# Squares of the keys two slots earlier, scaled keys one later, output transposes behind the inversion's products

## The chip, the cores and the metric

The kernel runs on one core of a Trainium2 chip. The metric is the device time of one execution in microseconds (us); the time before is the median of three runs. A profiled execution of the same program gives the trace that is read here. Engines are called PE (TensorE matmul), PEld (its weight loads), DVE (VectorE), ACT (ScalarE), POOL (GpSimd) and SP (SyncE, which issues the DMAs).

## The reference, cut to what matters

Two layers over 256 positions of width 2048. Each layer normalises, projects by one matrix, and feeds two groups of heads: RWKV-7 time mixing in both directions (16 heads of 64), and windowed attention. Both are gated, concatenated and projected back. The change is in the time mixing; cut to its core:

```python
kk = heads(kf * k_k)
kk = kk * lax.rsqrt(jnp.maximum(jnp.sum(kk * kk, -1, keepdims=True), 1e-24))
for d, rev in enumerate((False, True)):
    ...                                   # decay, a, kd by low-rank products
    y = y + wkv_scan(rh, heads(decay), kd, vh, kk, heads(a), rev)
    bonus = bonus + jnp.sum(rh * kd * rkf, -1, keepdims=True)
mu = jnp.mean(y, -1, keepdims=True)
var = jnp.mean(jnp.square(y - mu), -1, keepdims=True)
yn = (y - mu) * lax.rsqrt(var + LNX_EPS)
out = yn * lnx_g + lnx_b + bonus * vh
...
S = S * w_t - s_kk * (a_t * kk_t) + v_t * k_t     # one step of the scan
```

The squares of the scaled keys and their sum over a head are the first line's norm; the normed output `yn` is what the transposes turn back.

## The kernel before, in words

All activations lie transposed, channels on partitions. The big projections stream weights of 128 x 1024 floats. Each is split by ACT into a high part (`hi`, line 241) and by DVE into a low part (`lo`, line 243), and each of a projection's 16 steps is three matmuls (lines 311 to 313). PE is nearly always in this stream; everything else is put between its steps.

The time mixing works on eight pairs of heads per layer, with chunks of 64 positions. Three generators hold its steps, one step from one `yield` to the next:

- `scan_p` (line 710): squares of the keys (`sq` on ACT, in the trace `t`; high copy `mf` on ACT; low part `sl` on DVE), scaled keys `kkr` (line 722), head sums `pk` on PE (lines 706 and 727), reciprocal and `kd` on DVE (line 730), then decays, key and value products, `vt` and its copies `suv` (lines 795 and 798), and the bonus sums `pbn`.
- `scan_i`: the chunk matrices (line 829) and their inversion in six levels, each a pair of steps: products `pq` (line 927) with a copy `QF` on ACT, and products `pd` (line 936) with a predicated copy on DVE.
- `scan_b`: the chunk recurrence, then the norm of the outputs: squares on ACT (line 1031), a power on POOL, the product `ysq` on DVE (line 1035), the transposes (line 1040, in the trace `py<-C,ysq`), and the gate.

The function `window` (line 413) runs 64 steps of the projection stream in 11 slots, five or six in each. Ahead of a slot's steps it advances the generators that have that slot in their list, in the order in which `scans` gives them. Window w starts `scan_p` for pair w, goes on with it for pair w - 1, runs `scan_i` for w - 2 and w - 3, and `scan_b` for w - 3 and w - 4. A pair's own projections run in its window: keys end in slot 2, values in slot 5, receptance in slot 8, gate in slot 10. A layer has twelve windows with such work and one with attention alone.

PE's order is this program order exactly (`manual_schedule`). On ACT, DVE and POOL a scheduler orders by readiness and priority when the program is built; afterwards each engine keeps that order. Steps issued through `PA` and `PV` (line 256, the helper's line in the trace) keep their program order among themselves on ACT and on DVE; `high_priority` moves others ahead, all of `scan_b` among them. SP issues the weight loads, which wait for free buffers.

PSUM for these products comes from two pairs of banks in turn (`wpair`, `wbank`), so a product may wait until what was read from an earlier one is done. `kkr`, `mf` and `sl` have one buffer each, the tag `t1` (squares, and the gated outputs) three.

Of the kernel before, what the change touches and what calls it, by code (L numbers as in the profile page):

```python
# [9 lines left out]
F32 = mybir.dt.float32  # L10
# [6 lines left out]
ALU = mybir.AluOpType  # L17
# [25 lines left out]

SLOTS = 11

STAGE_P = (([8], [6, 7, 8, 10]), ([9], [0, 1, 3, 4, 5, 6, 7, 8, 9]))
STAGE_I = (list(range(SLOTS)), [0, 1, 2, 3, 4])
STAGE_B = (list(range(5, SLOTS)), list(range(SLOTS)))
ATT = [
    [3, 9],  # L50
    [1, 3, 5, 6, 8, 10],
# [82 lines left out]
def hybrid_trunk_kernel(ctx, tc, xT, wi, wv, wo, par, fing, dup, iup, sink, pos, cst, out):  # L134
# [24 lines left out]
    def st(tag, shape, dt=F32, bufs=1):  # L159
        return sp.tile([128, *shape], dt, tag=tag, name=tag, bufs=bufs)  # L160
# [97 lines left out]
    PA, PV = InTurn(A), InTurn(V)  # L258
# [415 lines left out]
    def layer(l):  # L674
# [33 lines left out]


        def scan_p(p, t):  # L710
            K, VV = t["k"], t["v"]
            two = lambda x: x.unsqueeze(1).to_broadcast([128, 2, T])
            dd = lambda x: x.rearrange("p (d x) -> p d x", d=2)
            c8 = lambda x: x.rearrange("p (n j) -> p n j", j=64)
# [2 lines left out]
            sq = st("t1", [T], bufs=3)  # L717
            PA.activation(sq, K, AF.Square, scale=prm(P_KK, p))
            square = (st("mf", [T], F32R), st("sl", [T], F32R))
            PA.activation(square[0], sq, AF.Copy)  # L720
            KR = st("kkr", [T])
            PA.activation(KR, K, AF.Identity, scale=prm(P_KK, p))
            yield
            PV.tensor_tensor(square[1], sq, square[0].bitcast(F32), op=ALU.subtract)
            yield
            pk = wbank("pk")
            head_sums(pk, square)
# [2 lines left out]
            PV.reciprocal(KD, pk[:, 0:T])  # L730
            PV.scalar_tensor_tensor(KD, KD, 1e24, KR, op0=ALU.min, op1=ALU.mult)
            yield
# [40 lines left out]
            PA.activation(BK8[64:128, :, 0, :], BK8[64:128, :, 2, :], AF.Copy)  # L773
            yield

            R = t["r"]
            MV = st("mv", [2, NC, 2, 64], bufs=3)
            kr4 = c4(KR)
            PV.scalar_tensor_tensor(MV[:, 0, :, 0, 1:64], PP[:, 0, :, 0:63], -1.0, kr4[:, :, 1:64], op0=ALU.mult, op1=ALU.mult)
# [6 lines left out]
            PV.tensor_tensor(km[:, 0:T], km[:, 0:T], km[:, T : 2 * T], op=ALU.add)  # L786
            PV.scalar_tensor_tensor(km[:, 0:T], km[:, 0:T], prm(P_RK, p), R, op0=ALU.mult, op1=ALU.mult)
            yield
            PV.tensor_tensor(MV[:, :, :, 1, :], c4(R).unsqueeze(1).to_broadcast([128, 2, NC, 64]), PP, op=ALU.mult)
            SUV = st("suv", [2, NC, 2, 64], bufs=3)  # L790
# [263 lines left out]
        def scans(w):  # L1054

            gens = []
            prep = [(1, STAGE_P[1]), (0, STAGE_P[0])]
            stages = [(lag, scan_p, at[0]) for lag, at in prep]
            stages += [(4, scan_b, STAGE_B[1]), (3, scan_i, STAGE_I[1]), (2, scan_i, STAGE_I[0])]
            stages += [(3, scan_b, STAGE_B[0])]  # L1060
            stages += [(lag, scan_p, at[1]) for lag, at in prep]
            for lag, scan, at in stages:
                p = w - lag
                if 0 <= p < NP:
                    if (scan, p) not in chains:
                        chains[scan, p] = scan(p, L.ts[p])
                    gens.append((chains[scan, p], at))
            return gens
# [75 lines left out]
        for w in range(NP + 2):  # L1144
            window(64, *scans(w), *([(setup_, ROT.get(w, [2, 5, 9, 9]))] if l == 0 else []))
        att = attend()
        window(64, *scans(NP + 2), (att, ATT[0]))
        window(64, *scans(NP + 3), (att, ATT[1]))
        window(64, (att, ATT[2]))
        for _ in att:  # L1150
# [130 lines left out]
```

## Time and profile before

| | |
|---|---|
| median of three runs | 1194.66 us (1192.85 to 1195.58) |
| the profiled execution | 1198.96 us |
| its span, first to last instruction | 1197.2 us |
| mean granted PE clock | 0.987 |
| PE busy | 1159.4 us, 97% |
| PEld busy | 1084.0 us, 91% |
| DVE busy | 909.8 us, 76% |
| ACT busy | 778.6 us, 65% |
| DMA queue of the weights, share of 16 engines | 42.9% |

In the trace's lines an operation is given as out<-in by the program's tile names; `L706` is line 706 of the kernel. A timeline's line begins with its start and its duration in us, and a bracket at its end gives the idle time of the engine before it and what ended that.

### The profile page before, as it was taken

The numbers are of one execution on the slowest core, as the hardware profiler recorded it, in microseconds if no ns is written. First come the engines' busy times: TensorE is split into PE (matmuls) and PEld (weight loads), VectorE is DVE, ScalarE is ACT, GpSimd is POOL, SyncE is SP. The second block draws the span as 40 slices with busy tenths as digits, with TensorE's granted clock in tenths as the row PEclk, the third lists the DMA queues.
The fourth block names the chain that finished last, engine by engine and source line by source line (L and its number), as shares of the span: only waits on it lengthen the run. The fifth ranks groups of instructions, "written<-read, shape, count | busy, mean of one in ns | idle before, by whom it ended". The sixth has DMA issues, their size and how long they took to land.

```text
span 1197.2 us, 38092 instructions
## 1 busy us (share of the span) xinstructions
PE 1159.4 (97%) x16151; PEld 1084.0 (91%) x16151; DVE 909.8 (76%) x2017; ACT 778.6 (65%) x1955; POOL 22.2 (2%) x23
## 2 busy tenths in 40 slices
PE   8999999999999999999999999999999999999996
PEld 6988898889899988999999889898889999989996
DVE  6888978888777677856668888877887766786554
ACT  6657767776775667655556577867776666675553
POOL 0000000000000000000000000000000000000000
PEclk8999999999999999999999999999999999999998
DMA  7543333333233433477655343333333344345663
GB/s 255 163 148 127 110 119 98 121 98 114 90 108 123 136 116 117 140 222 246 203 186 181 117 136 105 110 115 108 114 97 108 116 139 133 98 147 184 209 191 122
DMA packets 60410, 166.63 MB, mean 139 GB/s; under 512 B 7728, under 2 KB 22736, under 8 KB 60240
## 3 DMA queue, kind: packets, MB, share of 16 engines
q1 hardware_dynamic: 60240, 164.21, 42.9%
q8 instruction: 126, 2.06, 0.7%
q14 instruction: 44, 0.36, 0.1%
HBM read 157.37 MB, written 4.19 MB: 135 GB/s over the span
## 4 chain that ended last, share of the span: by engine, by line
PE 69%; issue 14%; ACT 9%; DVE 5%; DMA 2%; SPq 0%; POOL 0%; POOLq 0%; DVEq 0%; ACTq 0%
PE pm L311 17%; PE pm L313 14%; PE pm L312 14%; PE pg L829 3%; ACT hi L241 3%; PE pcc L992 2%; PE py L1004 1%; PE py L977 1%; PE pd L936 1%; PE pcc L1020 1%; DVE kd L256 1%; DVE lo L243 1%; PE pcc L1010 1%; PE pq L927 1%; ACT suv L798 1%
## 5 line engine op out<-in xcount | busy, mean ns | idle before, releaser
L243 DVE TENSOR_TENSOR lo<-raw,hi 128x512 fp32r<-128x512 f32 x560 | 370.8, 686 | 123.7 <-ACT hi L241 118.5
L241 ACT ACTIVATE hi<-raw 128x512 fp32r<-128x512 f32 x560 | 330.3, 624 | 202.9 <-PE pm L312 110.7
L311 PE MATMUL pm<-XHa,hi 128*128 128x256 f32 x832 | 248.7, 299 | 1.7 <-ACT XHa L203 1.1
L311 PE MATMUL pm<-XHb,hi 128*128 128x256 f32 x832 | 244.1, 293 | 0.1
L312 PE MATMUL pm<-XLa,hi 128*128 128x256 f32 x832 | 236.2, 284 | 0.5 <-DVE XLa L204 0.3
L313 PE MATMUL pm<-XHb,lo 128*128 128x256 f32 x832 | 234.3, 282 | 1.7 <-DVE lo L243 1.7
L313 PE MATMUL pm<-XHa,lo 128*128 128x256 f32 x832 | 235.3, 283 | 0.0
L312 PE MATMUL pm<-XLb,hi 128*128 128x256 f32 x832 | 234.2, 282 | 0.0
L311 PEld LDWEIGHTS pm<-XHa,hi 128*128 128x128 f32 x832 | 158.9, 191 | 14.1 <-issue 3.2
L311 PEld LDWEIGHTS pm<-XHb,hi 128*128 128x128 f32 x832 | 157.5, 189 | 6.1 <-ACT hi L241 0.3
L312 PEld LDWEIGHTS pm<-XLa,hi 128*128 128x128 f32 x832 | 159.4, 192 | 1.1 <-DVE XLa L204 1.1
L313 PEld LDWEIGHTS pm<-XHb,lo 128*128 128x128 f32 x832 | 157.5, 189 | 2.1 <-DVE lo L243 2.1
L313 PEld LDWEIGHTS pm<-XHa,lo 128*128 128x128 f32 x832 | 159.2, 191 | 0.0
L312 PEld LDWEIGHTS pm<-XLb,hi 128*128 128x128 f32 x832 | 157.7, 190 | 0.3 <-DVE XLb L204 0.3
L1015 ACT ACTIVATE suv<-pcc 64x128 f32<-64x128 f32 x128 | 34.5, 270 | 72.9 <-PE pcc L1013 49.3
L311 PE MATMUL pm<-MHa,hi 128*128 128x256 f32 x256 | 72.2, 282 | 0.0
L313 PE MATMUL pm<-MHa,lo 128*128 128x256 f32 x256 | 72.0, 281 | 0.2 <-DVE lo L243 0.2
L312 PE MATMUL pm<-MLb,hi 128*128 128x256 f32 x256 | 71.9, 281 | 0.0
L311 PE MATMUL pm<-MHb,hi 128*128 128x256 f32 x256 | 71.9, 281 | 0.0
L313 PE MATMUL pm<-MHb,lo 128*128 128x256 f32 x256 | 71.9, 281 | 0.0
L312 PE MATMUL pm<-MLa,hi 128*128 128x256 f32 x256 | 71.9, 281 | 0.0
L311 PEld LDWEIGHTS pm<-MHa,hi 128*128 128x128 f32 x256 | 48.4, 189 | 0.9 <-issue 0.8
(291 smaller groups left out, 2320.7 us busy)
## 6 DMA issues: line engine op xcount, KB each, us to landing
raw<-wi SPq DMA_DIRECT2D x207, 512.0 KB
raw<-wo SPq DMA_DIRECT2D x64, 512.0 KB
raw<-wv SPq DMA_DIRECT2D x8, 512.0 KB
rrot<-u SPq DMA_DIRECT2D x80, 32.0 KB
vg<-xT SPq DMA_DIRECT2D x16, 128.0 KB
xd<-vg SPq DMA_DIRECT2D x16, 128.0 KB
vg<-xd SPq DMA_DIRECT2D x16, 128.0 KB
g<-dup SPq DMA_DIRECT2D x16, 97.0 KB
```

The costliest lines, as they stand in the source:

```text
L241: A.activation(hi[:, q], raw[:, q], AF.Copy)
L243: V.tensor_tensor(lo[:, q], raw[:, q], hi[:, q].bitcast(F32), op=ALU.subtract)
L256: return lambda *a, **k: tc.keep_in_program_order(getattr(self.engine, name)(*a, **k))
L311: PE.matmul(pm, wh, rh[:, kk, :], start=(kk == 0), stop=False)
L312: PE.matmul(pm, wh, rl[:, kk, :], start=False, stop=False)
L313: PE.matmul(pm, wl, rh[:, kk, :], start=False, stop=(kk == 15))
L798: A.activation(pick(SUV, half[1 - h], q * 128 + h * 64, [NC * 128, 2], [256, 2], [1, 64]), vt[half[q], h, 0:128].rearrange("p (b x) -> p b ...
L829: PE.matmul(pg[:, h, c * 128 : (c + 1) * 128], BK[half[h], d, c, 1 - h : 3 - h, :].rearrange("p s j -> p (s j)"), MV[half[h], d, c].rearra ...
L927: PE.matmul(narrow(pq[:, d], h ^ d, c), hq(AB, d, c, h), sub(TC, h, d, c, d * b), start=True, stop=True)
L936: PE.matmul(narrow(pd[:, d], h, c), hx(TT, d, c, h), sub(QF, h ^ d, d, c, d * b), start=True, stop=True)
L992: PE.matmul(pc[half[h], 0, d, :], GE[h][r, d, ci[d], 0, :], SUV[r, d, ci[d], h, :], start=True, stop=True)
L1015: A.activation(here(h), pc[half[h], 1], AF.Copy)
```

## The change

Three things move; what is computed stays the same.

- `scan_p` for the newest pair had its first step (square, high copy, scaled keys) in slot 6 and its second (low part) in slot 7. Now the square and its high copy are a step in slot 4, the low part is one in slot 5, and the scaled keys are a step of their own in slot 7. The head sums stay in slot 8, ahead of the other work of that slot. The value tile is fetched later in the function, since in slot 4 it doesn't exist yet.
- `scan_b` for the oldest pair had slot 7 (its transposes and the copy behind them) in the same list as its other late slots, ahead of `scan_i`. Slot 7 is now a list of its own behind both `scan_i` entries.
- The value `VV` is read from the pair's tiles together with `R`.

```diff
-STAGE_P = (([8], [6, 7, 8, 10]), ([9], [0, 1, 3, 4, 5, 6, 7, 8, 9]))
+STAGE_P = (([8], [4, 5, 7, 8, 10]), ([9], [0, 1, 3, 4, 5, 6, 7, 8, 9]))
 STAGE_I = (list(range(SLOTS)), [0, 1, 2, 3, 4])
-STAGE_B = (list(range(5, SLOTS)), list(range(SLOTS)))
+STAGE_B = (list(range(5, SLOTS)), [i for i in range(SLOTS) if i != 7], [7])
...
-            K, VV = t["k"], t["v"]
+            K = t["k"]
...
             PA.activation(square[0], sq, AF.Copy)
+            yield
+            PV.tensor_tensor(square[1], sq, square[0].bitcast(F32), op=ALU.subtract)
+            yield
             KR = st("kkr", [T])
             PA.activation(KR, K, AF.Identity, scale=prm(P_KK, p))
-            yield
-            PV.tensor_tensor(square[1], sq, square[0].bitcast(F32), op=ALU.subtract)
             yield
             pk = wbank("pk")
...
-            R = t["r"]
+            R, VV = t["r"], t["v"]
...
-            stages += [(3, scan_b, STAGE_B[0])]
+            stages += [(4, scan_b, STAGE_B[2]), (3, scan_b, STAGE_B[0])]
```

## The prediction

> **What bounds the kernel now.** I read the page first, then the list of what TensorE waited for, then the timelines of PE, ACT and DVE in one steady stretch and in two early ones.
>
> ```profile
> span 1197.2 us, 38092 instructions
> ...
> PE 1159.4 (97%) x16151; PEld 1084.0 (91%) x16151; DVE 909.8 (76%) x2017; ACT 778.6 (65%) x1955; POOL 22.2 (2%) x23
> ```
>
> PE is the bound: 1197.2 - 1159.4 = 37.8 us of idle time is all that reordering can win, beside time in which PE runs slowly. The profiled run took 1198.96 us, 1.76 more than its span and 4.30 (0.36%) more than the median of 1194.66; I work on the span and take the saving off the median.
>
> ```profile
> PE pk L706 <- DVE sl L256: 14.7, 13, 2.6
> PE py L1040 <- DVE ysq L256: 3.6, 4, 2.5
> PE pm L313 <- DVE lo L243: 1.9, 3, 1.2
> PE pd L936 <- DVE kd L256: 1.9, 8, 0.4
> ```
>
> The columns are us in total, times, longest. The first row is the low part of the squared keys (`sl`, line 724, recorded at helper line 256), for which the head sums `pk` at the start of slot 8 wait. The second is the transposes of the normed outputs (line 1040). Both are what the change moves. Where the 14.7 us lie: in windows 3 to 6 of layer 0 (130 to 290 us), in windows 3 to 7 of layer 1 (700 to 910 us), and in windows 1 and 2 of layer 1 (650 to 700 us), in this order:
>
> ```profile
> PE pk L706 <- DVE sl L256: 3.4, 4, 1.0
> PE pk L706 <- DVE sl L256: 3.2, 5, 0.8
> PE pk L706 <- DVE sl L256: 3.9, 2, 2.2
> ```
>
> One steady window (layer 1), PE, then ACT, then DVE:
>
> ```profile
> 804.81 0.28 PE L313 MATMUL pm<-XHa,lo 128*128 128x256 f32 x1
> ...
> 808.48 0.56 PE L1040 MATMUL py<-C,ysq 64*64 64x64 f32 x12
> ...
> 812.20 0.28 PE L706 MATMUL pk<-mf,BONES 128*128 128x256 f32 x1
> 813.23 0.38 PE L706 MATMUL pk<-sl,BONES 128*128 128x256 f32 x1 [0.76 <-DVE sl L256]
> ...
> 815.57 0.28 PE L313 MATMUL pm<-XHa,lo 128*128 128x256 f32 x1
> 815.69 0.28 PE L311 MATMUL pm<-XHa,hi 128*128 128x256 f32 x1
> ...
> 817.42 0.30 PE L936 MATMUL pd<-QF,tt 64*64 64x32 f16 x16 [0.28 <-DVE kd L256]
> ```
> ```profile
> 802.01 1.15 ACT L241 ACTIVATE hi<-raw 128x512 fp32r<-128x512 f32 x2
> ...
> 804.71 1.15 ACT L241 ACTIVATE hi<-raw 128x512 fp32r<-128x512 f32 x2 [0.53 <-ACT rh L994]
> ...
> 808.44 0.50 ACT L256 ACTIVATE t<-kr,PR 128x256 f32<-128x256 f32 x1
> 808.98 0.42 ACT L256 ACTIVATE mf<-t 128x256 fp32r<-128x256 f32 x1
> ...
> 814.22 0.63 ACT L241 ACTIVATE hi<-raw 128x512 fp32r<-128x512 f32 x1
> ```
> ```profile
> 802.67 1.30 DVE L243 TENSOR_TENSOR lo<-raw,hi 128x512 fp32r<-128x512 f32 x2 [1.12 <-ACT hi L241]
> ...
> 808.01 0.42 DVE L256 TENSOR_TENSOR ysq<-py,yv 128x256 f32<-128x256 f32 x1
> ...
> 812.77 0.41 DVE L256 TENSOR_TENSOR sl<-t,mf 128x256 fp32r<-128x256 f32 x1
> ...
> 814.88 0.69 DVE L243 TENSOR_TENSOR lo<-raw,hi 128x512 fp32r<-128x512 f32 x1 [0.57 <-ACT hi L241]
> 815.61 1.76 DVE L256 RECIPROCAL kd<-pk 128x256 f32<-128x256 f32 x1
> ```
>
> Two matmuls of a stream start 0.12 us apart (815.57, 815.69), so `pk`'s second one was due at 812.20 + 0.12 = 812.32 and came 0.91 late. What the reader should see is that two more waits stand right behind it. The weights' low half ends at 814.88 + 0.69 = 815.57, the very moment at which its matmul starts; and the reciprocal ends at 815.61 + 1.76 = 817.37, just before `pd` starts at 817.42, for `pd` takes the PSUM pair that `pk` held. Both hang on the ACT instruction at 814.22, and ACT has no gap worth naming from 804.71 to there. So the 0.91 us is not free: ACT in slots 5 to 8 is almost as late as `sl`.
>
> **The early windows** (1 and 2 of layer 0): ACT and PE.
>
> ```profile
> 71.88 0.62 ACT L241 ACTIVATE hi<-raw 128x512 fp32r<-128x512 f32 x1
> ...
> 105.35 1.16 ACT L798 ACTIVATE suv<-vt 64x256 f32<-64x256 f32 x3
> ```
> ```profile
> 72.13 0.39 PE L706 MATMUL pk<-sl,BONES 128*128 128x256 f32 x1 [2.58 <-DVE sl L256]
> ...
> 73.44 0.42 PE L313 MATMUL pm<-XHa,lo 128*128 128x256 f32 x1
> 73.66 0.41 PE L311 MATMUL pm<-XHa,hi 128*128 128x256 f32 x1
> ...
> 106.20 0.38 PE L706 MATMUL pk<-sl,BONES 128*128 128x256 f32 x1 [1.64 <-DVE sl L256]
> 106.56 0.30 PE L927 MATMUL pq<-tv,AB 64*64 64x32 f16 x16
> ```
>
> The waits are longer, and from 73.44 on the matmuls start 0.22 us apart instead of 0.12. The busy times by stretches say why (PE busy and its count first; the granted clock behind POOL):
>
> ```profile
> 69.70:73.10 3.40, 0.97 (x8) 0.97 (x9) 3.23 (x8) 2.76 (x8) 0.00 (x0) 1.00 0.13 49
> 73.13:76.54 3.41, 3.41 (x18) 3.41 (x18) 3.41 (x6) 1.15 (x2) 0.00 (x0) 0.50 0.47 154
> 103.85:107.26 3.41, 1.77 (x42) 1.41 (x41) 3.12 (x7) 3.33 (x10) 0.00 (x0) 1.00 0.36 133
> 107.26:110.67 3.41, 3.41 (x18) 3.41 (x17) 2.70 (x5) 2.82 (x6) 0.00 (x0) 0.50 0.46 155
> 308.65:312.06 3.41, 3.41 (x60) 3.14 (x61) 3.28 (x10) 3.07 (x9) 0.00 (x0) 0.50 0.02 5
> 660.22:663.63 3.41, 3.28 (x15) 3.29 (x16) 3.31 (x6) 1.63 (x3) 0.00 (x0) 0.50 0.34 80
> 690.94:694.35 3.41, 1.77 (x16) 1.56 (x15) 2.92 (x9) 3.31 (x10) 0.00 (x0) 1.00 0.51 159
> ```
>
> Stretches in which PE worked only 0.97 and 1.77 of 3.4 us were followed by 3.41 us at half clock. Four such stretches stand inside the kernel, three behind a `pk` wait and one (308.65) behind the 2.5 us `py` wait. The wait at 690.94 to 694.35 left PE the same 1.77 and brought none, so about half busy is the edge.
>
> **The change, part by part.** No instruction is added or removed; PE, ACT and DVE work stays 1159.4, 778.6 and 909.8 us, and no DMA moves.
>
> (1) Square and its high copy go from slot 6 to slot 4, `sl` from slot 7 to slot 5. The key's projection ends in slot 2, so the input is there. `sl` is then some two slots early and the whole `pk` wait goes; what counts is the next wait. In the steady window the two ACT pieces held 808.44 to 809.30 = 0.86 us of ACT's unbroken row; they land behind the first pair of 802.01, where ACT has a gap of 0.53 to fill, so ACT is 0.86 - 0.53 = 0.33 later at 804.71 and 0.53 earlier at 814.22. `lo`, the reciprocal and `pd` follow by that much; DVE's 0.41 us of `sl` leaves the same row and arrives before `ysq`. PE thus gains about 0.55 of 0.91 and waits the rest at `lo` and `pd`. Bounds per window: 0.25 (the scheduler puts other ACT work into the place) and 0.91. For windows 4 to 6 and 4 to 7: 7 x 0.55; for the two windows 3, of which layer 1's has a short wait, 0.7 each: **5.2 us** (2.3 to 8).
>
> (2) In window 1 the next wait is the weights' high half, 71.88 + 0.62 = 72.50, needed six matmuls (0.7 us) behind a `pk` that is on time (72.13 + 0.39 - 2.58 = 69.94 for its end). It stands at the end of ACT's row and moves up by 0.8 (square and copy gone) to 1.4 (the scaled keys, 0.5, too, since they now follow `ip` in ACT's program order). In window 2 it is the last copy out of `vt` (`suv`, 105.35 + 1.16 = 106.51), whose PSUM pair `pq` takes at 106.56: again 0.8 to 1.4. I take 1.3 for each of four early windows, nearer the upper row since ACT has room in slots 4 and 5 there: **5.2 us** (3.2 to 7.7, the waits themselves).
>
> (3) The half clock. A stretch costs 3.41 x (1 - 0.12 / 0.22) = 1.55 us if nothing else holds PE; I take 1.4. Waits cut to 0.9 to 1.3 us leave PE over 2.1 of 3.41 us of work, above the 1.77 at which it tips. Three stretches: **4.2 us** (0 to 6.2, the fourth included). The Trainium skill (TensorE: Matmul & The Clock Gate, "What's actually happening") says that the gate falls back only after an idle window of about 3.4 us. The rows above disagree, since 0.97 and 1.77 us of work did not hold it; by the page's rule this term would be nothing and the sum 10.8 us (a rival below). The same section says that the windows run freely, and with that the two stretches of 1.77 us agree: the same load tipped once and once not.
>
> (4) Scaled keys from slot 6 to slot 7: 0.5 us of ACT within the same row, read next by DVE behind the reciprocal at the end of slot 8. Nothing on the path; if they came after the reciprocal, 0.4 us of DVE (bounds 0 and 0.4), nobody on PE waits for them until the next window.
>
> (5) Transposes behind the 16 products of the slot, in windows 4 to 9; in the two last windows there are none and nothing moves. `pd` runs while `ysq` is made, but `ysq` comes 0.33 later since `sl` now precedes it on DVE (0.41 less the overlap). Of PE's wait (3.6 us in all, 2.5 of it once) `pd` fills 0.25 and `ysq` gives it back, except in window 7 of layer 0, where DVE waits for ACT anyway: **0.4 us** (-1 to 3.6). The copy behind them on ACT, and DVE's two steps on it, come no later than before, with ACT 0.5 us ahead.
>
> Sum: 5.2 + 5.2 + 4.2 + 0.4 = **15.0 us**; 1198.96 - 15.0 = 1184.0 for a profiled run, 1194.66 - 15.0 = **1179.7** at the median.
>
> **Rivals.** *All waits go*: ACT and DVE follow fully; 14.7 + 3.6 + 1.9 of `pd` and four half-clock stretches at 1.5 = 26 us, 1168.5. Against it: ACT's row without gaps. *The half clock returns*: the 1.3 us that may be left of the early waits, split in two pieces, tip the clock as 1.64 us did, and (3) is lost: 10.8 us, 1183.9. For it: 1.77 us of work did not always suffice; against: over 2.1 would now stand in a stretch. *The wait moves on*: only the lower bounds, 2.3 + 3.2 with the half clock back in two early windows (1.4 left) minus 1 in (5): 6 us, 1188.7. For it: `lo` and `pd` have no slack today. *Nothing*: the scheduler sets the squares late once more, or `lo` takes every wait over: 1192.3 to 1197.0. Against it: the helper keeps the squares ahead of slot 5's ACT steps in program order. *Slower*: in slots 4 and 5 squares and `sl` stand before the weight halves, and PE waits there instead. The first `lo` of the pair at 802.67 ends at about 803.36; PE wants it at 804.81: 1.45 us of slack. Squares 0.92 and `sl` 0.41 make 1.33, just inside; with the output squares (about 0.9 on ACT) also put first it is 2.2, 0.8 too late in 14 windows, 11 us, and three new half-clock stretches 4.2, with (2) kept and (1) lost: 11 + 4.2 - 5.2 - 4.2 = 6 us slower, 1200.5. It decides once 1.45 us are used up.
>
> **How the numbers follow.** Forecast (12 to 19 us saved) 0.45; half clock returns (9 to 12) 0.13; all waits 0.07; wait moves on 0.18; nothing 0.10; slower 0.07. A measurement here tells 0.2% (2.4 us) from no change. Faster 0.45 + 0.13 + 0.07 + 0.18 = 0.83, same 0.10, slower 0.07. Range: the forecast's own is 1176 to 1183; with its neighbours on both sides 1171 to 1190.
>
> **What would show it.** Right: no PE wait on `sl`; PE waits on `lo` (L313), `kd` (L936) and `suv` (L927) grown to 4 to 7 us together; the half clock only at start, end and near 300 us; `hi` of slot 8 some 0.5 us earlier against `pk`. Wrong: PE waiting for `lo` in slots 5 or 6, half clock in new places, or a total PE idle time that fell by less than 5 us.

## The result, and the profile after

The changed kernel takes **1181.7 us** at the median of four runs (1180.42 to 1182.11) against 1194.66; the ratio is 0.9892 (95% interval 0.9874 to 0.9909), that is 10.9 to 15.1 us saved. The prediction was 1179.7 us. Of the runs below, one of the kernel before (1961 us) and two of E7's six (3474 and 3673 us, the profiled one among them) were lengthened by a disturbance, and no median, ratio or trace reading uses them.

The page of the changed kernel, its span and the first of its busy times:

```profile
span 1178.6 us, 38072 instructions
...
PE 1149.2 (98%) x16151; PEld 1076.2 (91%) x16151; DVE 906.1 (77%) x2017; ACT 777.5 (66%) x1955; POOL 21.7 (2%) x23
```

PE's idle time is 1178.6 - 1149.2 = 29.4 us, 8.4 less than before, and its busy time fell by 10.2 us though it does the same work. So about half of what the profiles show is not waiting but speed. The profiled execution after took 1180.42 us, 1.3 under its median, and the one before 1198.96, 4.3 over its own: the two profiles differ by 18.5 us, the medians by 13.0, and the profiles must not be read as if all of their difference came from the change.

What PE waited for, in the changed kernel (us in total, times, longest):

```profile
PE pd L937 <- DVE kd L256: 5.8, 10, 0.7
PE pm L313 <- DVE lo L243: 2.2, 4, 1.2
PE pd L937 <- ACT tt L899: 2.0, 1, 2.0
...
PE pq L928 <- ACT suv L799: 1.3, 2, 0.6
```

The wait for `sl`, 14.7 us before, is gone. The wait of `pd` for the reciprocal's PSUM pair grew from 1.9 to 5.8 us; the one for `lo` hardly grew (1.9 to 2.2).

A window's work on the scan opens with the products `pza` of the low ranks (line 691), so the time from one window's first `pza` to the next one's is the window's length on PE. The group of them in the trace, before and then after; "first and last start" is its third pair of numbers:

```profile
L691 PE MATMUL pza<-TW,duh x32: 278/283/388, 48.7 to 905.0; 97*128 97x256 f32 x32
```
```profile
L691 PE MATMUL pza<-TW,duh x32: 278/283/387, 47.1 to 886.5; 97*128 97x256 f32 x32
```

From first to last that is 856.3 us before and 839.4 after, 16.9 less. By window, from the starts in PE's timelines:

| window | before, us | after, us | difference |
|---|---|---|---|
| layer 0: 1, 2, 3 | 29.64, 35.78, 37.70 | 27.05, 34.00, 36.99 | -2.59, -1.78, -0.71 |
| layer 0: 4, 5, 6 | 41.89, 41.91, 41.90 | 41.22, 41.07, 41.21 | -0.67, -0.84, -0.69 |
| layer 0: 7 | 44.52 | 43.66 | -0.86 |
| layer 1: 1, 2, 3 | 29.22, 34.30, 37.48 | 26.67, 33.82, 36.74 | -2.55, -0.48, -0.74 |
| layer 1: 4, 5, 6, 7 | 41.56, 41.57, 41.56, 41.58 | 40.89, 40.89, 40.91, 40.89 | -0.67, -0.68, -0.65, -0.69 |

That is 14.6 us in the windows that the change touches. Of the rest, 2.2 us lie in layer 0's output projection, which it does not touch. There the profiled run of before ran its matmuls more slowly at full granted clock. Eighty us of it (PE busy and count first, the clock behind POOL), before and then after:

```profile
524.00:604.00 80.00, 79.79 (x664) 79.41 (x664) 51.23 (x97) 40.96 (x83) 0.00 (x0) 1.00 0.71 220
```
```profile
512.00:592.00 80.00, 80.00 (x683) 80.00 (x682) 52.60 (x100) 42.39 (x85) 0.00 (x0) 1.00 0.72 229
```

664 matmuls against 683 in the same time, with 0.2 us of waits. Another 1.6 us were lost by before's profile ahead of the first window. These two make 3.8 of the 5.5 us by which the profiles differ more than the medians do.

One steady window (layer 1, the one that starts at 763.39) in the changed kernel; PE, then ACT, then DVE:

```profile
795.66 0.28 PE L706 MATMUL pk<-mf,BONES 128*128 128x256 f32 x1
795.78 0.28 PE L706 MATMUL pk<-sl,BONES 128*128 128x256 f32 x1
...
800.27 0.30 PE L937 MATMUL pd<-QF,tt 64*64 64x32 f16 x16 [0.54 <-DVE kd L256]
```
```profile
785.54 0.50 ACT L256 ACTIVATE t<-kr,PR 128x256 f32<-128x256 f32 x1
...
792.90 1.14 ACT L241 ACTIVATE hi<-raw 128x512 fp32r<-128x512 f32 x2
...
796.27 0.50 ACT L256 ACTIVATE kkr<-kr,PR 128x256 f32<-128x256 f32 x1
```
```profile
789.86 0.42 DVE L256 TENSOR_TENSOR sl<-t,mf 128x256 fp32r<-128x256 f32 x1
...
796.47 0.68 DVE L243 TENSOR_TENSOR lo<-raw,hi 128x512 fp32r<-128x512 f32 x1
...
797.41 0.68 DVE L243 TENSOR_TENSOR lo<-raw,hi 128x512 fp32r<-128x512 f32 x1
798.01 0.41 DVE L256 TENSOR_TENSOR ip<-th,ip 128x256 fp32r<-128x256 f32 x1
798.46 1.76 DVE L256 RECIPROCAL kd<-pk 128x256 f32<-128x256 f32 x1
```

`sl` is ready 5.4 us before `pk` wants it, and `pk`'s two matmuls are 0.12 apart. What the reader should see next is where the two `hi` of slot 8 went: they end at 792.90 + 1.14 = 794.04, 1.62 us before `pk` starts (795.66), where the one that counted before ended at 814.85, 2.65 us behind its `pk` (812.20). That is 4.3 us, not 0.5. Only this second half of the pair moved: the first started 2.9 us ahead of `pk` before (809.30) and starts 2.8 ahead now. ACT is no longer what comes late. DVE is: the sums of `pk` are done at about 796.1, and the reciprocal starts at 798.46 because two `lo`, `ip` and two steps of the gated outputs stand before it, in a row that has run without a gap since 786.60. `pd` pays 0.54 us for it.

The half clock, in stretches of the changed kernel:

```profile
73.00:76.50 3.50, 3.20 (x27) 3.00 (x26) 3.50 (x7) 2.28 (x5) 0.00 (x0) 1.00 0.78 249
107.30:110.70 3.40, 3.17 (x56) 2.94 (x55) 2.87 (x7) 2.08 (x6) 0.00 (x0) 1.00 0.51 153
301.00:304.40 3.40, 3.40 (x18) 3.40 (x17) 2.90 (x7) 3.32 (x10) 0.00 (x0) 0.50 0.00 0
...
660.20:663.60 3.40, 3.40 (x38) 3.20 (x37) 2.41 (x4) 2.74 (x5) 0.00 (x0) 1.00 0.19 61
```

The three stretches behind a `pk` wait are at full clock. The one near 300 us, window 7 of layer 0, stays; it now stands behind a wait of 2.0 us of `pd` for ACT's `tt`.

### The profile page after: what moved, and what is told of

It is laid out like the page before. It is cut to its first block, busy times and chain, and to the rows that moved or that the text cites. A ratio compares the mean times of both kernels' runs of the same rounds, so it can differ in the third digit from the quotient of the medians.

```text
span 1178.6 us, 38072 instructions
## 1 busy us (share of the span) xinstructions
PE 1149.2 (98%) x16151; PEld 1076.2 (91%) x16151; DVE 906.1 (77%) x2017; ACT 777.5 (66%) x1955; POOL 21.7 (2%) x23
## 5 line engine op out<-in xcount | busy, mean ns | idle before, releaser
L312 PE MATMUL pm<-XLa,hi 128*128 128x256 f32 x832 | 233.8, 281 | 0.5 <-DVE XLa L204 0.3
L311 PEld LDWEIGHTS pm<-XHa,hi 128*128 128x128 f32 x832 | 156.4, 188 | 15.1 <-issue 3.2
L312 PEld LDWEIGHTS pm<-XLa,hi 128*128 128x128 f32 x832 | 156.8, 188 | 1.0 <-DVE XLa L204 0.9
L313 PEld LDWEIGHTS pm<-XHa,lo 128*128 128x128 f32 x832 | 156.6, 188 | 0.9 <-DVE lo L243 0.9
```

The lines of the kernel that those rows point to most:

```text
L311: PE.matmul(pm, wh, rh[:, kk, :], start=(kk == 0), stop=False)
L312: PE.matmul(pm, wh, rl[:, kk, :], start=False, stop=False)
L313: PE.matmul(pm, wl, rh[:, kk, :], start=False, stop=(kk == 15))
```

## The experiments

Two readings of the steady windows were to be told apart. The first is the prediction's: behind `sl`, ACT's row is next (through `hi` and `lo`), and `pd` with it. The second is what the profile after suggests: ACT has slack now, and DVE's row up to the reciprocal binds (A2 where an expectation gives it a letter). E1 to E5 and E10 to E12 take the change apart; E6 to E9 load or unload one engine. "Ratio" is against the kernel before, run beside it on the same chip; runs of different batches are compared by their ratios.

**E1: the squares and the keys, not the transposes.** The whole change in `scan_p`, `STAGE_B` and the order of `scan_b` as before:

```diff
-STAGE_P = (([8], [6, 7, 8, 10]), ...
+STAGE_P = (([8], [4, 5, 7, 8, 10]), ...
...
 STAGE_B = (list(range(5, SLOTS)), list(range(SLOTS)))
```

> Squares, their low part and the scaled keys in their new slots, the output transposes where they were. Theory A (the head sums' wait is what the change earns, shared out over windows): 12 to 13 us faster than the kernel before, within 1 us of the whole change (0.989). Rival B (the transposes earn the 3.6 us that PE waited for them): only 9 us faster.

Measured: 1181.6 us, ratio 0.988 (0.9863 to 0.9897). The gain is whole without the transposes. `pd` waits for `kd` 5.3 us, as in the changed kernel; `py` waits for `ysq` 1.3 us, where it waits 0.4 in the changed kernel.

**E2: the transposes alone.**

```diff
-STAGE_B = (list(range(5, SLOTS)), list(range(SLOTS)))
+STAGE_B = (list(range(5, SLOTS)), [i for i in range(SLOTS) if i != 7], [7])
...
-            stages += [(3, scan_b, STAGE_B[0])]
+            stages += [(4, scan_b, STAGE_B[2]), (3, scan_b, STAGE_B[0])]
```

> Only the output transposes behind the inversion's products. Theory A: 0 to 1 us faster, no change that can be told. Rival B: 3 us faster or more.

Measured: 1194.08 us, ratio 0.999 (0.9977 to 1.0003): no change that can be told. The waits of PE:

```profile
PE pk L706 <- DVE sl L256: 12.7, 13, 2.4
PE pd L936 <- DVE kd L256: 3.6, 7, 0.7
...
PE py L1040 <- DVE ysq L256: 0.7, 3, 0.4
```

`py`'s wait shrinks from 3.6 to 0.7 us, and most of that comes back elsewhere: `pd` for `kd` 1.7 us more, `pd` for `tt` 1.8 us in window 7, where before `py` had waited 2.5.

**E3 and E4: the squares moved for some pairs only.** E3 moves squares and keys of pairs 1 and 2 (the early windows), E4 those of pairs 0 and 3 to 7; the transposes move in both.

```diff
+LATE_P = ([8], [6, 7, 8, 10])
+MOVED = (1, 2)
...
-            prep = [(1, STAGE_P[1]), (0, STAGE_P[0])]
+            prep = [(1, STAGE_P[1]), (0, STAGE_P[0] if w in MOVED else LATE_P)]
```

> The whole change, but the squares are moved for head pairs 1 and 2 of each layer alone. Theory A: 6 to 7.5 us faster than before, half clock gone behind these windows. Rival C (the half clock is all that is earned, the steady windows only hand the wait on): 11 to 13 us faster, nearly the whole gain.

> The whole change, but the squares are moved for pairs 0 and 3 to 7 and stay late for pairs 1 and 2. Theory A: 5.5 to 7 us faster, with the waits of 1.6 to 2.6 us and the half clock behind them still there. Rival C: under 2 us faster.

Measured: E3 1188.43 us, ratio 0.9939 (0.9926 to 0.9953), 6.8 us under before's 1195.2; E4 1187.1 us, ratio 0.9927 (0.9913 to 0.9942), 8.1 us under and 1 us more than expected. The two parts make 14.9 us together, and the whole 13.6 on the same chip (E1): within the intervals they add up, so the four early windows carry a little less than half of the gain.

E4 keeps the long early waits and so shows the half clock at work. The waits of windows 1 and 2 of layer 0, and below them two stretches around window 2 of layer 1:

```profile
PE pk L708 <- DVE sl L258: 4.0, 2, 2.3
```
```profile
681.00:684.40 3.40, 1.78 (x42) 1.43 (x41) 2.91 (x7) 3.32 (x9) 0.00 (x0) 1.00 0.22 84
684.40:687.80 3.40, 3.40 (x18) 3.40 (x18) 2.76 (x5) 2.87 (x7) 0.00 (x0) 0.50 0.47 153
```

The two waits of layer 0, 2.3 and 1.6 us, were followed by no half clock in this run, while before's profile had it behind both; the 1.6 us wait in layer 1 was followed by it here, and not in before's profile, with as much PE work ahead (1.78 and 1.77 us). One profile's list of stretches is a draw, not a property of the kernel.

**E5: the keys back in slot 6, the squares as in the change.**

```diff
-STAGE_P = (([8], [4, 5, 7, 8, 10]), ...
+STAGE_P = (([8], [4, 5, 6, 8, 10]), ...
```

> The whole change, but the scaled keys stay in slot 6, as a step of their own; squares in 4 and 5, transposes moved. As predicted (scaled keys behind ip free ACT for the weights' high half and the suv copies in the early windows): 1 to 2 us slower than the whole change, so 11 to 12 us faster than before. Rival E (the scaled keys' place doesn't matter): within 0.5 us of the whole change, 13 us faster.

Measured: 1183.46 us, ratio 0.9903 (0.9882 to 0.9924). `pq` now waits for the copies `suv` in ten windows and `pbn` for `ip` in the two windows 1:

```profile
PE pq L928 <- ACT suv L799: 4.7, 10, 1.0
...
PE pbn L706 <- DVE ip L256: 2.4, 2, 1.2
```

The early windows are 0.1 to 0.7 us longer for it. The steady ones are not (40.87 to 40.90 us in layer 1): with the keys' 0.50 us back ahead of `suv` (and behind both `hi`), PE waits 0.45 us there, and `pd`'s wait shrinks from 0.54 to 0.16. `pd` starts 4.61 us behind `pk` in both kernels, which is when the reciprocal lets it.

**E6 and E7: half a microsecond more for ACT, or for DVE.** Both work on the changed kernel: E6 makes the scaled keys twice (0.50 us of ACT in slot 7), E7 one of the first key products twice (0.41 us of DVE in slot 6).

```diff
             PA.activation(KR, K, AF.Identity, scale=prm(P_KK, p))
+            PA.activation(KR, K, AF.Identity, scale=prm(P_KK, p))
```
```diff
             PV.scalar_tensor_tensor(MV[:, 0, :, 0, 1:64], PP[:, 0, :, 0:63], -1.0, ...
+            PV.scalar_tensor_tensor(MV[:, 0, :, 0, 1:64], PP[:, 0, :, 0:63], -1.0, ...
```

> The whole change, with the scaled keys of slot 7 written twice on ACT, 0.5 us more of ACT per window in the place of the last suspected queue. Theory as predicted (ACT's unbroken row sets what is late next): 0.4 us in each of some 13 windows, 5 us slower than the whole change, so 8 us faster than before. Theory A2 (after the change DVE's row up to the reciprocal is the bound, ACT has slack): 0 to 1 us slower, 12 to 13 us faster than before.

> The whole change, with one 0.41 us product of slot 6 (its first, into mv) done twice on DVE. Theory A2: the reciprocal and the pd behind it come 0.33 us later in each of some 13 windows, 4 to 5 us slower than the whole change, 8 to 9 us faster than before. Theory as predicted (ACT): 0 to 1 us slower.

Measured: E6 1180.69 us, ratio 0.9879 (0.9858 to 0.99), no worse than the changed kernel's 0.9892, with steady windows of 40.88 to 40.90 us. E7 1184.92 us at the median of four, ratio 0.9916 (0.9891 to 0.9942), 4.2 us above E6 on the same chip (E6's runs go from 1179.41 to 1181.57, E7's from 1184.43 to 1186.09). E6's extra copy stands behind `ip`, and so behind both `hi` of the slot; what it shows is that ACT's row from there to `pd` has half a microsecond to spare. For the row up to `hi`, the profile after shows the slack: both are done at 794.04, and DVE first takes them up at 796.47. With these two the first reading falls, and E7 supports the second: 4.2 us over the ten windows that have the wait is 0.42 for each, the 0.41 us that was added. That it lies in these windows is inferred, since no trace of E7 is read.

**E8: the reciprocal before the second `lo`.** The changed kernel with other priorities on DVE:

```diff
-            with tc.high_priority(offset=PRIO_LO):
+            with tc.high_priority(offset=PRIO_LO if i == 0 else 30):
                 V.tensor_tensor(lo[:, q], raw[:, q], hi[:, q].bitcast(F32), op=ALU.subtract)
...
-            PV.reciprocal(KD, pk[:, 0:T])
+            with tc.high_priority(offset=36):
+                V.reciprocal(KD, pk[:, 0:T])
...
-            low(bonus, km[:, 0:T])
+            with tc.high_priority(offset=60):
+                V.tensor_tensor(bonus[:, 1], km[:, 0:T], bonus[:, 0].bitcast(F32), op=ALU.subtract)
```

> The whole change, with DVE's queue in slot 8 set as: low part of the bonus, first low weight half, reciprocal, second low weight half (by priorities; the work is the same). Theory A2: the reciprocal ends 0.6 us earlier, the 5.8 us that pd waited for kd nearly go, 3 to 5 us faster than the whole change, 16 to 18 us faster than before (ratio 0.985). Theory as predicted (ACT): no change against the whole change.

Measured: 1178.23 us, ratio 0.9857 (0.9834 to 0.9879), 5.2 us under E5 and 2.5 under E6 on the same chip. DVE in the same steady window as above (`pk` starts at 794.59 here):

```profile
796.07 0.68 DVE L243 TENSOR_TENSOR lo<-raw,hi 128x512 fp32r<-128x512 f32 x1
796.79 1.76 DVE L732 RECIPROCAL kd<-pk 128x256 f32<-128x256 f32 x1
798.46 0.63 DVE L243 TENSOR_TENSOR lo<-raw,hi 128x512 fp32r<-128x512 f32 x1
```

The reciprocal starts 2.20 us behind the start of `pk`, not 2.80; PE waits for `kd` nowhere longer than 0.09 us, and the steady windows are 40.47 us long against 40.89. That is the 0.42 us that the changed kernel still pays each time. The new order has a price in window 1 of each layer, where PE now waits 1.4 and 1.6 us for a `lo`, and 0.2 in the changed kernel.

**E9: E8, and the sine table's steps out of window 7.** Aimed at the one 2.0 us wait of `pd` for `tt` and the half clock behind it.

```diff
-ROT = {0: [2, 3], 1: [], 7: [2, 5, 7], 8: [1, 3], 9: []}
+ROT = {0: [2, 3], 1: [], 7: [2], 8: [5, 7], 9: []}
```

> e8's kernel, with the sine and cosine of the positions (and the table load that ACT makes for them) moved from window 7 to slots 5 and 7 of window 8 of layer 0, where no squares, keys or key norms of a new pair are made. If the wait of 2 us on ACT in slot 7 of window 7 and the half clock behind it come from that table load: 2 to 3.5 us faster than e8, 20 us faster than before (ratio 0.983). If the wait only moves to window 8: no change against e8.

Measured: **1175.71 us** (1174.9 to 1176.1), ratio 0.9829 (0.9807 to 0.9851): faster than both kernels. Seven us around the place, E9 and then the changed kernel:

```profile
297.00:304.00 7.00, 6.94 (x128) 6.58 (x124) 6.92 (x16) 6.16 (x16) 0.00 (x0) 1.00 0.23 75
```
```profile
297.00:304.00 7.00, 5.03 (x74) 4.64 (x73) 6.56 (x17) 6.91 (x21) 0.00 (x0) 0.79 0.24 77
```

What stood in front of `tt` is in ACT's rows, the changed kernel's first, then E9's: a table load, ahead of the sine and the cosine.

```profile
296.42 1.28 ACT L256 ACT_TABLE_LOAD   x1
```
```profile
334.33 1.28 ACT L256 ACT_TABLE_LOAD   x1
```

Window 7 of layer 0 goes from 43.66 to 40.48 us. In window 8, where the load is now, PE waits 1.1 us for `tt`, and the window's 64 stream steps take 41.63 us instead of 40.46: so 1.2 us moved along, and the rest and the half clock went.

**E10: the squares one slot later than in the change.** Square and high copy in slot 5, low part in 6, keys in 7.

```diff
-STAGE_P = (([8], [4, 5, 7, 8, 10]), ...
+STAGE_P = (([8], [5, 6, 7, 8, 10]), ...
```

> The whole change, but square in slot 5 and low part in slot 6, one slot later each. Theory A2 (sl has two slots to spare, DVE's row up to the reciprocal is the bound): within 1 us of the whole change, since the same work stands ahead of the reciprocal. If the place in slots 4 and 5 matters because ACT and DVE have room there: 2 to 5 us slower than the whole change.

Measured: 1194.33 us, ratio 0.9986 (0.9972 to 1.0). Nearly the whole gain is lost, far beyond both readings. The early windows keep theirs (27.53 and 33.91 us for windows 1 and 2 of layer 0, against 29.64 and 35.78 before); the steady windows are 42.11 to 42.17 us in layer 1, 0.6 longer than before. PE, then ACT, in the one that starts at 772.60:

```profile
801.86 0.30 PE L937 MATMUL pd<-QF,tt 64*64 64x32 f16 x16 [0.69 <-ACT tt L899]
802.55 0.68 PE L1041 MATMUL py<-C,ysq 64*64 64x64 f32 x16 [0.39 <-DVE ysq L256]
...
806.75 0.39 PE L706 MATMUL pk<-sl,BONES 128*128 128x256 f32 x1 [0.29 <-DVE sl L256]
```
```profile
799.33 0.51 ACT L256 ACTIVATE t<-kr,PR 128x256 f32<-128x256 f32 x1
...
800.31 0.42 ACT L256 ACTIVATE mf<-t 128x256 fp32r<-128x256 f32 x1
800.63 0.49 ACT L454 ACTIVATE vg<-u,DP 128x256 f32<-128x256 f32 x1
...
801.43 0.38 ACT L899 ACTIVATE tt<-pq 128x256 f16<-128x256 f32 x1
```

The two pieces, 0.93 us, now stand in front of `vg`, `QF` and `tt` of slots 5 and 6, and `pd` of slot 6 waits 0.69 us for `tt`; `ysq` waits on DVE behind `vg` and costs 0.39; and `sl`, in slot 6, stands so far back in DVE's order that `pk` waits for it again. Three waits, 1.37 us, in place of one of 0.54. Before the change the same two pieces came behind `tt`, in the change they come well ahead of it.

**E11: the keys alone.** The kernel before, with the scaled keys behind the low part in slot 7, squares, low part and transposes where they were.

```diff
             PA.activation(square[0], sq, AF.Copy)
-            KR = st("kkr", [T])
-            PA.activation(KR, K, AF.Identity, scale=prm(P_KK, p))
             yield
             PV.tensor_tensor(square[1], sq, square[0].bitcast(F32), op=ALU.subtract)
+            KR = st("kkr", [T])
+            PA.activation(KR, K, AF.Identity, scale=prm(P_KK, p))
```

> The kernel before with one thing moved: the scaled keys (0.50 us of ACT a window) are made behind the low part in slot 7, not behind the square in slot 6; square, high copy, low part and transposes stay where they were. The prediction's step (4): nothing, 1194 to 1196 us, ratio 0.998 to 1.002, and PE still waits some 14 us for sl. The reading of the profile after and of the run with the keys in slot 6 again (1.8 us between the two): the keys' place is worth a part of the gain by itself, since the weights' high half and the vt copies of slot 8 follow 0.5 us earlier; 1190 to 1193 us, ratio 0.996 to 0.998. A ratio below 0.995 would mean that the keys, not the squares, carry the change.

Measured: 1187.41 us, ratio 0.9935 (0.9915 to 0.9955), 8.6 us under before. That is beyond both readings, and past the ratio that was named as the sign of the keys, though the interval reaches 0.9955: the piece that I had priced at nothing brings some 60% of the gain when it is moved alone (0.65% of 1.08%). It does not carry the change by itself, since E5 has nearly the whole gain without it. Some 5.7 us of its windows' gain stand in the steady windows 4 to 6 and 4 to 7. Those of layer 1 are 40.79 to 40.84 us, shorter than in the changed kernel; the early ones keep most of their waits (2.0 us in window 1 of layer 1, 1.1 in window 2). Its wait for `sl`, then ACT in a steady window (the one that starts at 770.46, `pk` at 802.82):

```profile
PE pk L706 <- DVE sl L256: 7.1, 6, 2.0
```
```profile
799.04 0.50 ACT L256 ACTIVATE t<-kr,PR 128x256 f32<-128x256 f32 x1
...
800.96 1.14 ACT L241 ACTIVATE hi<-raw 128x512 fp32r<-128x512 f32 x2
...
803.57 0.40 ACT L256 ACTIVATE ip<-th 128x256 fp32r<-128x256 f32 x1
803.88 0.50 ACT L256 ACTIVATE kkr<-kr,PR 128x256 f32<-128x256 f32 x1
```

With the keys behind `ip`, both `hi` of slot 8 come ahead of `suv` and `pk`, though the squares are where they always were.

**E12: the squares in slot 4, the low part left in slot 7.**

```diff
-STAGE_P = (([8], [4, 5, 7, 8, 10]), ...
+STAGE_P = (([8], [4, 7, 7, 8, 10]), ...
```

> The changed kernel with the square and its high copy in slot 4 as there, but the low part sl (0.41 us of DVE) in slot 7, ahead of the scaled keys, as in the kernel before. It parts the two pieces that the run with squares in 5 and low part in 6 moved together. If ACT's place for the squares is what matters (its row in slots 5 and 6 leaves no room, its row in slot 4 does): no PE wait for tt in slot 6 of the steady windows, PE waits for sl by 0 to 0.5 us a window, 1181 to 1187 us, ratio 0.989 to 0.994. If it is the place of sl in DVE's row that matters: PE waits for sl by 0.7 to 1 us a window as before, 1190 to 1195 us, ratio 0.996 to 1.0.

Measured: 1184.17 us, ratio 0.9909 (0.9892 to 0.9926): the ratio that the first reading of it gave. Yet `pk` waits for `sl` by 0.7 us in the steady windows, which I had put to the other, so neither reading is right by itself. No wait for `tt` in slot 6. PE and DVE in the window that starts at 766.38:

```profile
799.89 0.39 PE L706 MATMUL pk<-sl,BONES 128*128 128x256 f32 x1 [0.70 <-DVE sl L256]
```
```profile
798.82 0.68 DVE L256 TENSOR_TENSOR mv<-kr,pp 128x512 f32<-128x512 f32 x1
799.42 0.41 DVE L256 TENSOR_TENSOR sl<-t,mf 128x256 fp32r<-128x256 f32 x1
```

`mf` has long been there. `sl` is late since it keeps its place in the program's order on DVE, behind the products of the keys (`mv` the last of them): it starts 0.52 us behind the start of `pk` (798.90), where it started 0.57 behind in the kernel before (812.77 against 812.20). These windows are still 0.2 us shorter than before, as the reciprocal no longer waits for a late `hi`.

The steady windows of layer 1 side by side (the middle ones, from one first `pza` to the next):

| kernel | squares, low part, keys in slots | us | PE waits in it |
|---|---|---|---|
| before | 6, 7, 6 | 41.57 | `sl` 0.76, `pd` 0.28 |
| E11 | 6, 7, 7 | 40.84 | `suv` 0.20, `sl` under 0.1 |
| E5 | 4, 5, 6 | 40.90 | `suv` 0.45, `pd` 0.16 |
| the change | 4, 5, 7 | 40.89 | `pd` 0.54 |
| E12 | 4, 7, 7 | 41.40 | `sl` 0.70 |
| E10 | 5, 6, 7 | 42.17 | `tt` 0.69, `ysq` 0.39, `sl` 0.29 |
| E8 | 4, 5, 7, other DVE order | 40.47 | none above 0.1 |

## Why the prediction was right, and where not

The time was right: 1181.7 us lies 2.0 above the forecast and inside its own range of 1176 to 1183; 13.0 us saved where 15.0 were forecast. Part of that is luck: by the profiles' windows, the early waits were worth half of their term, and the steady windows, window 7 and the half clock made up for it.

**Step (1), steady windows**: 5.2 us forecast; the nine windows 3 to 6 and 3 to 7 gave 6.3, about 0.65 to 0.84 each where 0.55 (0.7 for the windows 3) stood. The shape was right, since the 0.91 us did not come free and a wait of `pd` took the rest. The reason was wrong. I wrote that ACT would be 0.53 us earlier and that `lo`, the reciprocal and `pd` would follow by as much. The second `hi` came 4.3 us earlier, since the scheduler now places the pair together; why it does was not examined. E5 and E6 show that ACT could take another 0.5 us in these windows for nothing, and E7 and E8 that the rest hangs on DVE's row up to the reciprocal.

One of the two waits that I saw right behind `sl` was none. The low half that ended at 815.57, "the very moment" of a matmul, is the tile's second (the first ended at 809.95 + 0.69 = 810.64). Each half holds the columns of four steps, so the second is first read in the tile's fifth, at 818.72. E8 shows it: the fourth low matmul of the tile starts while the second `lo` (798.46) has not begun.

```profile
798.14 0.28 PE L313 MATMUL pm<-XHa,lo 128*128 128x256 f32 x1
```

That `lo` mattered only by standing in front of the reciprocal on DVE.

**Step (4), the scaled keys**: nothing, I wrote, since nobody on PE waits for them. This is the step that failed most, by E11: moved alone they bring 8.6 us at the median. I asked who waits for the instruction and not who stands behind it on its engine: ACT's `hi`, for which `lo`, the reciprocal and `pd` wait. It did no harm in the sum only because in the steady windows squares and keys do the same thing. Either one out of ACT's row ahead of `hi` suffices (E5 moves the squares and not the keys, E11 the keys only, and both reach 40.8 to 40.9 us), and both together add nothing, as DVE binds by then. Had the change been the keys alone, I would have missed it.

**Step (2), early windows, and step (3), the half clock**: 5.2 + 4.2 forecast, 7.4 measured in the four windows. Window 1 looks right in both layers, 2.6 us each against 1.3 + 1.4, and window 2 oversized, 1.78 in layer 0 and 0.48 in layer 1. E4 parts the two terms, for its run had the long waits without the half clock in three of the four windows: 27.81 and 27.69 us for the windows 1, 34.30 for window 2 of layer 0. Against the changed kernel that is 0.8, 1.0 and 0.3 us, with the 0.5 of layer 1's window 2, which had no half clock before, 2.6 us in all for the waits. So step (2) was twice too large, and the other 4.8 us are the half clock. I took one wait to be next, `suv`; the profile after has three there, and in both layers about the same:

```profile
PE pq L928 <- ACT suv L799: 0.6, 1, 0.6
PE pd L937 <- DVE kd L256: 0.5, 1, 0.5
PE pza L691 <- DVE kd L256: 0.3, 1, 0.3
```

(windows 1 to 3 of layer 1; the third stands at the start of window 2.) So the wait that moves on, a rival for the whole, is what happened in window 2, and it moved to DVE's reciprocal there too. Squares carry these windows: E11, which leaves them, saves 0.6 us in window 1 of layer 0 and 1.4 in that of layer 1, where its run had no half clock.

The 4.2 us of the half clock hold on average. Over the 55 runs of the kernel before that stood beside the experiments, the mean granted clock is 0.9890; over 15 of the changed kernel, E1 and E6 it is 0.9934. Half-clock time is twice the shortfall: 2 x 0.0110 x 1193.6 = 26.3 us against 2 x 0.0066 x 1179 = 15.6, so 10.7 us less, and with 1 - 0.12 / 0.22 of it lost, 4.9 us. What was argued from one profile, three stretches by name, was luck in its detail: E2 and E4 draw other ones under the same waits. The Trainium skill (TensorE: Matmul & The Clock Gate, "What's actually happening") has the gate fall back after an idle window of about 3.4 us; the rows here, E4's above, 1.78 us of work in 3.40 and then half clock, disagree, and its free-running windows agree with a draw.

**Step (5), transposes**: 0.4 us forecast; E2 measures 1.1 us with an interval that holds zero, and E1 has the whole gain without them. Right as far as it can be told. The 2.5 us in window 7 did not go, as I said; the wait now has the name `tt`, the table load stands in front of it, and moving it was worth 2 us in E9.

**The signs named ahead**: no wait on `sl` (right), half clock only at start, end and near 300 us (right in this run, save that its profile has no such stretch at the start), `lo`, `kd` and `suv` together 4 to 7 us (9.3, nearly all of the growth in `kd`), `hi` 0.5 us earlier (4.3).

**The slower rival** did not come about in slots 4 and 5, but E10 shows how near it was: one slot further on, squares and `sl` do stand before what PE wants next. I had placed it at the weight halves; there it is `tt`, and it costs the steady windows 0.6 us more than before.

What stays open is why the scheduler put the second `hi` late before and early after, and where E7's time lies. E11's steady windows with the changed kernel's early ones, that is, squares moved for pairs 1 and 2 and keys for all, was not tried. Nor was an order other than E8's for the reciprocal in E11.

## What to carry to other kernels

When an instruction is moved, price what stands behind it on its engine, not only who reads its result: half a microsecond that nobody waits for, in a row without gaps, held up everything after it. When two edits unload the same row, measure each alone, for the second may add nothing and the first may be the one that you priced at zero. And a step put earlier helps only where its engine has room: the same pieces in slot 4 of ACT's row gave a gain, in slot 5 longer steady windows than before, and in slot 6, with the keys out of the way, windows as short as in slot 4.

## What the hardware showed that I had not expected

The kernel's own scatter goes with the clock. Among the 55 runs of before, the 7 with a mean granted clock of 0.992 took 1192.1 us on average and the 18 with 0.988 took 1196.5: 4.4 us for 0.004 x 1193.6 x 2 = 9.5 us of half clock, or 1.6 us for a stretch of 3.41. The kernel with waits of 1.6 to 2.6 us has a standard deviation of 2.2 us from run to run (1191.6 to 1199.1), while the changed kernel, E1, E6 and E12, which have lost most of these waits, have 0.8 to 1.6 us, from 4 to 6 runs each. That the lost waits are the cause is likely but not shown.

Layer 0's output projection ran 2 to 3% slower in before's profile at a granted clock of 1.00 and with 0.2 us of waits (664 matmuls in 80 us, 683 after; E3's profile has 677). No run here shows why.
